# A hybrid decoder layer: PSUM tiles behind attention taken from the pool of the bank that the planner finds free, instead of from two pools in turn

## The chip, the cores and the metric

The kernel runs on one core of a Trainium2 chip. The engines named below are TensorE (PE, with PEld for its weight loads), VectorE (DVE), ScalarE (ACT), GpSimd (POOL) and SyncE (SP, which here only issues DMAs). TensorE writes its results to PSUM, which has eight banks; a tile of 128 x 512 float32 fills one bank. The metric is the time of one execution on the device in microseconds (us), the median of the runs.

## The reference

One layer of a hybrid decoder over 1024 positions of width 1024, in float32. Cut to what matters:

```python
h = rms_norm(x, norm_mix_pre)
q, k, v, cb, cc, cx, g_att, g_conv = split(h @ w_in)
o = stick_breaking_attention(heads(q), heads(k), heads(v))      # 8 heads of 64, causal
y_att = o @ w_att_branch
y_conv = (cb * causal_dwconv(cc * cx, conv_mix_w)) @ w_conv_branch
merged = sigmoid(g_att) * y_att + sigmoid(g_conv) * y_conv
x = x + rms_norm(merged @ w_out, norm_mix_post)
h = rms_norm(x, norm_ffn_pre)
a, g = split(causal_dwconv(h @ w_up, conv_ffn_w))                # 2 x 2816 columns
x = x + rms_norm((gelu(g) * a) @ w_down, norm_ffn_post)
```

## The kernel before

Every product is made of float16 halves: a float32 operand is split into a high and a low half, and three of the four products of halves are added up in PSUM, so that a product of 128 x 512 with an inner size of 512 is twelve matmuls (the three `PASSES` times four). The large products, up and down projection among them, go by a scheme of seven block products in place of eight, for which sums and differences of blocks of the activations and of the weights are made ahead.

The program has three parts, each put in order by a planner (`Plan`, at the end of the file). A part adds jobs (`pl.add`) with an engine, a cost, the tiles that they read and write and, for many, a due time; TensorE's large products keep the order in which they were added (`seq=True`), and the rest is fitted in. `Plan.order` walks a clock of its own, takes for each engine the job that can start first, and keeps for each pool of tiles a sorted list `free` of the times at which its buffers come free. The result is one fixed order for each engine. Which buffer a tile really gets is not part of the plan: when the program is written down, a job asks its pool for a tile (`Buf.t` calls `make`), the pool takes that one of its own buffers which comes free first in the library's own reckoning, and semaphore waits are added so that the new tile is not written before the last reader of the old one is through.

PSUM stands in two pools. While attention runs, `pm` (3 banks, L138) holds projections, and another pool holds attention's scores and outputs. Behind attention that other pool is closed, and `pz` (5 banks) takes its place; `pm` is kept as `self.pm3`. Both plans behind attention reckon with one pool `pm` of eight banks. The class `Ring` (L1815) joins the two for them: it has a list of eight entries, five times `pz` and three times `pm`, and each new tile is asked of the next entry, round and round, whatever that pool holds just then. `bank` (L739) is the one place where `rest` (the two parts behind attention) asks for a PSUM tile.

The stretch that matters below is the passage from the output projection to the up projection. The rows of the sequence stand in eight tiles of 128 positions, taken in the order 0, 4, 1, 5, 2, 3, 6, 7 (`TORDER`). For each tile, `out_proj` multiplies by `w_out` into two banks (`py`), adds the residual and makes the normed rows `hn`. Then the blocks of the activations that the up projection needs are made, in two ways:

- Tiles 3 and 7 are transposed on TensorE (L1317) into two banks, `pt`; for tile 7, ScalarE copies each into `hb` (L1357), and the differences `tb` are made from `hb`, split (L1350, L1351) and put into `hB` and `hT`.
- The others (`TURNED`) go through the DMA. For tiles 4, 5, 6 `heavy` (L1282) makes differences in two PSUM tiles `tp` on VectorE (L1289), ScalarE and VectorE split them into high and low halves in an SBUF tile `n` (L1270, L1271), and a transposing DMA from SyncE's queue puts each half into `hB` or `hT` (L1265). Two SBUF tiles `n` are used for a tile of positions; the first is written a second time after its first transposes were read.

The up projection takes its weights in 22 steps `u0` to `u21`. Each has raw weights (`ws_u`), a scale that goes through a one-column matmul `pr_u` (L813), four float16 weight tiles `wh_u` (L825 the high half on ScalarE, L827 the low half on VectorE), and three accumulators in PSUM: `pu0a`, `pu0b`, `pu0c` for step 0 (L1425). Products 1 and 2 of a step, into `b` and `a`, need only tiles 0 to 3; 5, 6, 7, 3 and 4 need blocks of tiles 4 to 7. For steps 0, 1 and 2 the products 1 and 2 are put ahead of the others (`PRE`), around the last transposes. TensorE's order there is: `pu1a`, transposes of tile 7 into `pt7_0` and `pt7_1`, `pu2b`, `pr_u` of step 3, `pu2a`, then `pu0c` (product 5) and twice `pu0b` (products 6 and 7).

Of the kernel before, what the change touches and what calls it, by code (L numbers as in the profile page):

```python
# [47 lines left out]
class Layer:  # L48
    def __init__(self, tc, a):
        self.tc, self.nc, self.a = tc, tc.nc, a  # L50
# [82 lines left out]
    def mixer(self, mid):  # L133
        tc, nc, a = self.tc, self.nc, self.a
        hT = self.hp.tile([P, 2, KD, T], F16, tag="hT", name="hT")
        with ExitStack() as ph1:
            pha = ph1.enter_context(ExitStack())
            pm = self.top.enter_context(tc.tile_pool(name="pm", bufs=3, space=bass.MemoryType.PSUM))  # L138
# [12 lines left out]
            if True:  # L151
# [34 lines left out]
                with tc.manual_schedule(engines={ET.PE, ET.DVE, ET.Activation, ET.SP, ET.Pool}):  # L186
# [3 lines left out]
                    vec, act, pe, pool = nc.vector, nc.scalar, nc.tensor, nc.gpsimd  # L190
                    NOTE = lambda: Buf(None, lambda: {})

                    def given(p, tile, avail=0.0):
                        b = Buf(p, None)
                        b.tile, b.avail = tile, avail
                        pl.caps[p] -= 1
                        return b
# [50 lines left out]
                    for c in range(2):  # L248
                        M(0.94, lambda c=c: pe.matmul(gpb.t.rearrange("p k t -> p (k t)")[:, ds(c * NH, NH)], on1[0:1, :],
                                                      gr[0:1, ds(c * NH, NH)], start=True, stop=True), [one_row, g_row], [(gpb, str(c))])  # L250
                    M(0.3, lambda: pe.matmul(ps2.t[:, 0:2], self.ones[0:1, :], g_c.t["g16"][0:1], start=True, stop=True),
                      [g_c], [ps2])
                    def norm(tt):
                        r, x = Buf("sm", lambda: self.small(f"r_pre{tt}")), xs[tt]
                        A(1.25, lambda: self.sumsq(xt[tt], r.t[:, 0:1], f"n_pre{tt}"), [x], [r])
                        V(0.15, lambda: vec.tensor_scalar(r.t[:, 1:2], r.t[:, 0:1], 1.0 / D, EPS, ALU.mult, ALU.add), [], [r])
                        pl.add("G", 0.6, lambda: pool.tensor_tensor(r.t[:, 2:3], r.t[:, 1:2], self.neghalf, ALU.pow), [], [r])
                        g = gpb if tt < 2 else gbb
                        V(1.28, lambda: vec.scalar_tensor_tensor(
                            xt[tt], xt[tt], r.t[:, 2:3], g.t.rearrange("p k t -> p (k t)") if tt < 2 else gb,  # L260
                            ALU.mult, ALU.mult), [r, g], [x])
# [412 lines left out]
                    for name in FILL:  # L674
                        which, j = name[:-1], int(name[-1])
# [5 lines left out]
                    k = 0  # L681
# [34 lines left out]
                    for b in [*(o16b[j] for j in range(4)), *(uf[j] for j in range(4)), *sig.values(), *(w for w, _ in wa), *yb.values(),  # L716
# [7 lines left out]

        self.xp = self.top.enter_context(tc.tile_pool(name="xp", bufs=4))
        self.h7p = self.top.enter_context(tc.tile_pool(name="h7p", bufs=1))
        self.pz = Ring((self.top.enter_context(tc.tile_pool(name="pz", bufs=5, space=bass.MemoryType.PSUM)), 5),
                       (self.pm3, 3))
        dram = self.dram = self.top.enter_context(tc.tile_pool(name="dram", bufs=1, space=bass.MemoryType.DRAM))
        self.x2 = [a["out"][ds(tt * P, P), :] for tt in range(self.DIRECT)] + \  # L730
            [dram.tile([P, D], F32, tag=f"x2_{tt}", name=f"x2d_{tt}") for tt in range(self.DIRECT, 8)]
# [3 lines left out]
    pz, DIRECT, dsums = None, 7, {}  # L735
# [1076 lines left out]
            pl.emit()  # L1812


class Ring:  # L1815


    def __init__(self, *pools):
        self.order, self.n = [p for p, k in pools for _ in range(k)], 0

    def tile(self, *a, **kw):
        p = self.order[self.n % len(self.order)]
        self.n += 1
        return p.tile(*a, **kw)


class Buf:
    def __init__(self, pool, make):
        self.pool, self.make, self.tile, self.log, self.left, self.avail = pool, make, None, [], 0, 0.0

    @property
    def t(self):
        if self.tile is None:
            self.tile = self.make()
        return self.tile

# [12 lines left out]
class Plan:  # L1849
# [29 lines left out]
    def order(self):  # L1879
        for j in reversed(self.jobs):  # L1880
            own = min([k.late for k in j.outs] + [j.due + j.lag + j.cost, self.now]) - j.lag - j.cost
            j.late = min(own, j.late) if j.seq else own
        free = {p: [0.0] * n for p, n in self.caps.items()}
        for j in self.jobs:
            j.n = len(j.deps)
            j.t0 = max([0.0] + [b.avail for b in j.bufs])
            for b in j.bufs:
                b.left += 1
                b.begun = b.tile is not None
        eng = {e: self.begin.get(e, 0.0) for e in self.LAG}  # L1890
        seq = [j for j in self.jobs if j.seq]
        pos = 0
        ready = {e: [j for j in self.jobs if j.eng == e and not j.n and not j.seq] for e in eng}
        dma, out, todo = self.loaded, [], len(self.jobs)
        while todo:
            best = None
            for e, now in eng.items():
                c = ready[e]
                if e == "PE" and pos < len(seq) and not seq[pos].n:
                    c = c + [seq[pos]]  # L1900
                pick = None
                for j in c:
                    t = max(now, j.t0 + j.rest, j.late - j.ahead)
                    for b in j.bufs:
                        if b.pool and not b.begun:
                            t = max(t, free[b.pool][0] + j.slack if free[b.pool] else 1e9)
                    key = (max(t, now + 0.05), j.late - (100 if e == "PE" and not j.seq else 0))
                    if t < 1e8:
                        if pick is None or key < pick[0]:
                            pick = key, t, j  # L1910
                if pick and (best is None or pick[1] < best[0]):
                    best = pick[1], e, pick[2]
            assert best, "no job can run"
            t, e, j = best
            todo -= 1
            if j.seq:
                pos += 1
            else:
                ready[e].remove(j)
            end = t + j.cost  # L1920
            eng[e] = end
            done = end + j.lag
            if hasattr(j, "load"):
                dma = max(dma, t + (1.9 if e == "SP" else 2.4)) + j.load
                done = dma + self.landed
            for b in j.bufs:
                if b.pool and not b.begun:
                    free[b.pool].pop(0)
                b.begun = True
                b.left -= 1  # L1930
                b.end = max(getattr(b, "end", 0.0), done)
                if b.pool and not b.left:
                    free[b.pool] = sorted(free[b.pool] + [b.end])
            for k in j.outs:
                k.n -= 1
                soon = self.own is not None and k.eng == e and not hasattr(j, "load")
                k.t0 = max(k.t0, end + self.own.get(e, 0.05) if soon else done if k.deps[j] else end)
                if not k.n and not k.seq:
                    ready[k.eng].append(k)
            out.append((t, len(out), j))  # L1940
        self.span, self.eng = max(eng.values()), eng
        return [j for _, _, j in sorted(out, key=lambda x: x[:2])]
# [46 lines left out]
```

## Time and profile before

| | |
|---|---|
| median of 3 runs | 1254.32 us (1254.06 to 1255.73) |
| profiled execution | 1258.49 us; its span, from first to last instruction, 1256.8 us |
| granted clock, mean over the span | 0.995 |
| ScalarE busy | 857.0 us, 68% |
| GpSimd busy | 86.1 us, 7% |
| HBM read and written | 92.88 MB and 37.75 MB |

The page's second part shows where in the span an engine is busy, in forty slices; a digit is the busy share in tenths. The twenty-first slice (about 628 to 660 us) holds the passage described above.

```profile
PE   9999999999999999999989999999999999999997
DVE  7988889857998675659869998699689869959866
PEclk9999999999999999999989999999999999999999
```

TensorE is busy almost throughout; the one digit below 9 ahead of the end is in that passage, and the granted clock dips in the same slice. Time that another engine stands idle costs nothing while TensorE is busy.

### The profile page before, as it was taken

To read this page: it belongs to the slowest core of one execution; us is meant where nothing else is said; L and a number is where in the kernel's file an instruction comes from. 1 tells how busy PE (TensorE), PEld (TensorE's weight loads), DVE (VectorE), ACT (ScalarE), POOL (GpSimd) and SP (SyncE) were. 2 spreads that over 40 slices of the span, in tenths; PEclk is the share of its full clock that TensorE was granted. 3 is DMA by queue.
4 is the path that set the end of the run, shared out by engine and by line. 5 is a ranking of instruction groups with operands and counts; after the bars stand their busy time and mean duration, and the time that the engine had idled before them with its cause. 6 is when DMAs were issued, how large, how long until landed. Compare 5 with 4: busy or idle time off the path is not lost.

```text
span 1256.8 us, 16464 instructions
## 1 busy us (share of the span) xinstructions
PE 1237.9 (98%) x6065; PEld 560.6 (45%) x6065; DVE 1014.5 (81%) x1599; ACT 857.0 (68%) x1250; POOL 86.1 (7%) x113
## 2 busy tenths in 40 slices
PE   9999999999999999999989999999999999999997
PEld 4444444444444444444434444444444444444443
DVE  7988889857998675659869998699689869959866
ACT  7766666736758465855647679678768967878424
POOL 1100000000000000002100001001200300111003
PEclk9999999999999999999989999999999999999999
DMA  8755677661223122657844105414930971594608
GB/s 277 158 135 104 143 134 177 150 135 35 67 84 118 34 73 70 227 168 167 220 116 137 61 14 212 190 34 82 251 103 6 200 197 34 94 257 140 180 1 134
DMA packets 148931, 160.80 MB, mean 128 GB/s; under 512 B 114425, under 2 KB 114553, under 8 KB 148850
## 3 DMA queue, kind: packets, MB, share of 16 engines
q1 hardware_dynamic: 138480, 123.05, 34.9%
q0 software_dynamic: 10368, 36.70, 14.1%
q8 instruction: 47, 0.77, 0.3%
q14 instruction: 34, 0.28, 0.1%
q10 hardware_dynamic: 2, 0.00, 0.0%
HBM read 92.88 MB, written 37.75 MB: 104 GB/s over the span
## 4 chain that ended last, share of the span: by engine, by line
PE 45%; DVE 2%; ACT 1%; issue 1%; DMA 1%; POOL 1%; POOLq 0%; DVEq 0%; ACTq 0%
PE pq L1584 12%; PE pd L1654 2%; PE pu2b L1425 1%; PE pu20b L1425 1%; PE pu19b L1425 1%; PE pu8b L1425 1%; PE pu6b L1425 1%; PE pu16b L1425 1%; PE pu12b L1425 1%; PE pu4b L1425 1%; PE pu3b L1425 1%; PE pu21b L1425 1%; PE pu13b L1425 1%; PE pu10b L1425 1%; PE pu18b L1425 1%
## 5 line engine op out<-in xcount | busy, mean ns | idle before, releaser
L1425 PEld LDWEIGHTS <-wh_u 128*128 128x128 f16 x1848 | 180.0, 98 | 222.6 <-issue 10.0
L825 ACT ACTIVATE wh_u<-ws_u,sc_u 128x1024 f16<-128x1024 f32 (+1 forms) x66 | 66.4, 1009 | 35.4 <-PE pr_dn L813 7.5
L994 PEld LDWEIGHTS <-wh_g 128*128 128x128 f16 x588 | 57.0, 98 | 68.9 <-issue 0.5
L1229 PE MATMUL py<-wo,m 128*128 128x512 f16 x384 | 83.3, 379 | 0.0
L1588 ACT ACTIVATE st<-pq,sd 128x512 f32<-128x512 f32 x112 | 74.8, 696 | 12.2 <-PE pq L1584 9.5
L827 DVE SCALAR_TENSOR_TENSOR wh_u<-ws_u,sc_u,wh_u 128x1024 f16<-128x1024 f32 (+1 forms) x66 | 72.5, 1104 | 10.2 <-ACT wh_u L825 9.7
L791 POOL DMA_DIRECT2D acc<-st x56 | 43.7, 781 | 435.8 <-ACT st L1588 435.8
L624 DVE TENSOR_TENSOR_SCAN e<-e,mask 128x512 f32<-128x512 f32 (+3 forms) x64 | 48.7, 808 | 13.3 <-ACT e L617 13.3
L1229 PEld LDWEIGHTS <-m 128*128 128x128 f16 x384 | 37.4, 98 | 44.9
L1457 DVE SCALAR_TENSOR_TENSOR ug<-cg,cw_g,ug 128x1023 f32<-128x1023 f32 (+1 forms) x44 | 56.3, 1279 | 1.3 <-ACT ug L1455 1.1
L1457 DVE SCALAR_TENSOR_TENSOR ua<-ca,cw_a,ua 128x1023 f32<-128x1023 f32 (+1 forms) x44 | 56.3, 1279 | 1.1 <-ACT ua L1455 1.1
L617 ACT ACTIVATE e<-z,cz 128x1024 f32<-128x1024 f32 (+3 forms) x48 | 42.2, 896 | 20.4 <-PE z L595 14.9
L66 ACT ACTIVATE jk_u<-ws_u 128x1024 bf16<-128x1024 f32 x44 | 46.5, 1056 | 11.8 <-DMA ws_u<-w_up_nt 11.7
L638 ACT ACTIVATE w<-e 128x1024 f16<-128x1024 f32 (+3 forms) x48 | 38.8, 837 | 12.6 <-DMA wt<-w 6.3
L459 PE MATMUL pcc<-hT,wh_cc 128*128 128x512 f16 x192 | 44.5, 380 | 0.8 <-ACT u L575 0.8
L459 PE MATMUL pk<-hT,wh_k 128*128 128x512 f16 x192 | 43.1, 379 | 0.0
L459 PE MATMUL pq<-hT,wh_q 128*128 128x512 f16 x192 | 43.0, 379 | 0.0
L1584 PE MATMUL pq<-wq,fx 128*128 128x512 f16 x192 | 42.8, 379 | 0.0
L1584 PE MATMUL pq<-wq,fy 128*128 128x512 f16 x192 | 42.7, 379 | 0.0
L924 PE MATMUL pywc<-p,wh_wc 128*128 128x512 f16 x192 | 42.6, 379 | 0.0
L1584 PE MATMUL pq<-wq,fs 128*128 128x512 f16 x192 | 42.2, 379 | 0.0
L624 DVE TENSOR_TENSOR_SCAN e<-e,cr,mask 128x512 f32<-128x512 f32 x32 | 39.8, 1273 | 1.0 <-ACT e L617 0.8
(795 smaller groups left out, 2734.0 us busy)
## 6 DMA issues: line engine op xcount, KB each, us to landing
acc<-st POOLq DMA_DIRECT2D x56, 512.0 KB, 6.1
ws_u<-w_up_nt SPq DMA_DIRECT2D x44, 512.0 KB, 3.6
ds<-w_down SPq DMA_DIRECT2D x18, 512.0 KB, 15.0
wt_g<-w_in_nt SPq DMA_DIRECT2D x14, 512.0 KB, 3.5
x<-x SPq DMA_DIRECT2D x8, 512.0 KB, 8.1
wr_wo<-w_out SPq DMA_DIRECT2D x8, 512.0 KB, 3.6
ws_wo<-w_out SPq DMA_DIRECT2D x8, 512.0 KB, 4.4
xr<-x SPq DMA_DIRECT2D x8, 512.0 KB, 4.5
```

Source lines behind the costliest of these rows:

```text
L66: self.nc.scalar.activation(self.junk(f"jk_{name}"), src, AF.Square, accum_out=acc)
L459: pe.matmul(ps.t, w.t[:, wi, ds(k * P, P)], hT[:, hi, k, ds(c * NH, NH)], start=k == 0 and p == 0, stop=k == KD - 1 and p == 2)
L624: vec.tensor_tensor_scan(x, x, m[:, ::-1], ONE if diag else cr.t[:, h:h + 1], ALU.mult, ALU.max)
L791: j = pl.add(eng, 0.45 if eng == "SP" else 1.14, lambda: e.dma_start(dst(), srcf(), **kw), r, [b] if w is None else w, ahead=AHEAD["load"] ...
L825: A(C["As" if big else "Ash"], lambda: act.activation(dst.t[:, 0, dsl], src.t[:, ssl], AF.Copy, scale=sb.t["s"]), [(src, sreg), sb], [(dst ...
L827: V(C["V" if big else "Vh"], lambda: vec.scalar_tensor_tensor(dst.t[:, 1, dsl], src.t[:, ssl], sb.t["s"], dst.t[:, 0, dsl], ALU.mult, ALU. ...
L994: pe.matmul(b.t, p.w[wt].t[:, wi, ds(wc * NH + k * P, P)], block(i, h, k), start=first and n == 0, stop=n == 3 * KH - 1, skip_group_check= ...
L1229: pe.matmul(b.t, m16[k].t[:, h_, ds(tt * P, P)], wo[k].t[:, w_, sl], start=k == 0 and p == 0, stop=k == 7 and p == 2)
L1425: pe.matmul(b.t, p.w[wt].t[:, wi, ds(wc * NH + k * P, P)], block(i, h, k), start=first and n == 0, stop=n == 3 * KH - 1, skip_group_check= ...
L1457: V(C["V"], lambda lag=lag: vec.scalar_tensor_tensor(u.t[:, lag:], c.t[:, :T - lag], sm.t[:, 2 - lag:3 - lag], u.t[:, lag:], ALU.mult, ALU ...
L1584: pe.matmul(b.t, fa[p].t[:, h, ds(fo * NH + tt * P, P)], wa[p].t[:, x, ds(wo * NH, NH)], start=first and n == 0, stop=n == 5, skip_group_c ...
L1588: A(C["Ah"], lambda tt=tt, b=b, st=st: act.activation(st.t[:, tt % 2, :], b.t, AF.Copy, scale=q.sd.t[:, 0:1]), [b, q.sd], [(st, str(tt % 2 ...
```

## The change

`Ring` goes. In its place, `Plan.order` keeps beside each free time of the pool `pm` which of the two PSUM pools the bank belongs to: five of the eight start as `pz` and three as `pm`. When a job takes a bank, the mark of the bank that came free first is stored in the tile's `Buf` (`which`), and when the tile is released the mark goes back into the list with the time. `Buf.t` sets `Banks.want` to that mark just before the tile is made, and `Banks.tile` asks that pool. Costs, due times and the free times are untouched.

```diff
-        self.pz = Ring((self.top.enter_context(tc.tile_pool(name="pz", bufs=5, space=bass.MemoryType.PSUM)), 5),
-                       (self.pm3, 3))
+        self.pz = Banks(self.top.enter_context(tc.tile_pool(name="pz", bufs=5, space=bass.MemoryType.PSUM)), self.pm3)
...
-class Ring:
+class Banks:
+    want = 0
     def __init__(self, *pools):
-        self.order, self.n = [p for p, k in pools for _ in range(k)], 0
+        self.pools = pools
     def tile(self, *a, **kw):
-        p = self.order[self.n % len(self.order)]
-        self.n += 1
-        return p.tile(*a, **kw)
+        return self.pools[Banks.want].tile(*a, **kw)
...
     def t(self):
         if self.tile is None:
+            Banks.want = self.which
             self.tile = self.make()
...
-        free = {p: [0.0] * n for p, n in self.caps.items()}
+        free = {p: [(0.0, p == "pm" and n == 8 and i > 4) for i in range(n)] for p, n in self.caps.items()}
...
-                            t = max(t, free[b.pool][0] + j.slack if free[b.pool] else 1e9)
+                            t = max(t, free[b.pool][0][0] + j.slack if free[b.pool] else 1e9)
...
-                    free[b.pool].pop(0)
+                    b.which = free[b.pool].pop(0)[1]
...
-                    free[b.pool] = sorted(free[b.pool] + [b.end])
+                    free[b.pool] = sorted(free[b.pool] + [(b.end, b.which)])
```

The order of instructions is the same on every engine, row by row. What differs in the built program is where 230 PSUM tiles lie, and with that the waits. (Line numbers behind the first edit are lower by one after the change.) In the passage described above the banks are these; a bank's former holder is the tile that must have been read before the new one is written:

| tile | bank, former holder, before | bank, former holder, after |
|---|---|---|
| `tp6_0` | 7 (`pz`), `py3_1` | 2 (`pm`), `tp5_0` |
| `tp6_1` | 5 (`pz`), `pr_u1` | 7 (`pz`), `pr_u1` |
| `pt7_0` | 3 (`pz`), `pr_u2` | 6 (`pz`), `pr_u2` |
| `pt7_1` | 3 (`pz`), `pt7_0` | 0 (`pm`), `pr_dn0` |
| `pu2b` | 3 (`pz`), `pt7_1` | 1 (`pm`), `pu0a` |
| `pr_u3` | 7 (`pz`), `tp6_0` | 6 (`pz`), `pt7_0` |
| `pu2a` | 1 (`pm`), `pr_dn0` | 0 (`pm`), `pt7_1` |
| `pu0c` | 2 (`pm`), `pu0a` | 2 (`pm`), `tp6_0` |

The first place is TensorE from the end of `pu1a` to the start of `pu2b`. A name in brackets is the semaphore that the row waits for: that of ScalarE (Activation), VectorE (DVE) or of a DMA queue. Before:

```order
L1425 MATMUL pu1a<-hT,wh_u_0_5767 128x512
L1317 MATMUL pt_0_5993<-ident,hn_5865 128x128 [waits DVE_49]
L1317 MATMUL pt_0_5993<-ident,hn_5865 128x128 x3
L1317 MATMUL pt_1_6001<-ident,hn_5865 128x128 [waits Activation_49]
L1317 MATMUL pt_1_6001<-ident,hn_5865 128x128 x3
L1425 LDWEIGHTS wh_u_0_5987
L1425 MATMUL pu2b<-hT,wh_u_0_5987 128x512 [waits Activation_49]
```

And after, where the wait of the second transposes is gone, the wait of `pu2b` is for VectorE (the reader of `pu0a`), and its weight's own wait, which the other had covered, stands by itself:

```order
L1424 MATMUL pu1a<-hT,wh_u_0_5767 128x512
L1316 MATMUL pt_0_5993<-ident,hn_5865 128x128 [waits DVE_49]
L1316 MATMUL pt_0_5993<-ident,hn_5865 128x128 x3
L1316 MATMUL pt_1_6001<-ident,hn_5865 128x128 x4
L1424 LDWEIGHTS wh_u_0_5987 [waits Activation_49]
L1424 MATMUL pu2b<-hT,wh_u_0_5987 128x512 [waits DVE_49]
```

In both, the third matmul of `pu2b` also waits for VectorE, for the low half of the weight. The second place is TensorE from the one-column product of step 3 (`pr_u`) to `pu0c`. Before:

```order
L813 LDWEIGHTS ones
L813 MATMUL pr_u_6032<-rb_u_5990,ones 128x1 [waits DVE_49]
L1425 LDWEIGHTS wh_u_0_5987
L1425 MATMUL pu2a<-hT,wh_u_0_5987 128x512
...
L1425 LDWEIGHTS wh_u_2_5268 [waits DMAHW5_49,DMAHW3_49]
L1425 MATMUL pu0c<-hB,wh_u_2_5268 128x512 [waits Activation_49]
L1425 LDWEIGHTS wh_u_2_5268 [waits DMAHW6_49]
L1425 MATMUL pu0c<-hB,wh_u_2_5268 128x512 [waits DMAHW4_49]
```

After:

```order
L812 LDWEIGHTS ones
L812 MATMUL pr_u_6032<-rb_u_5990,ones 128x1 [waits Activation_49]
L1424 LDWEIGHTS wh_u_0_5987
L1424 MATMUL pu2a<-hT,wh_u_0_5987 128x512 [waits Activation_49]
...
L1424 LDWEIGHTS wh_u_2_5268 [waits DMAHW5_49,DMAHW3_49]
L1424 MATMUL pu0c<-hB,wh_u_2_5268 128x512 [waits DVE_49]
L1424 LDWEIGHTS wh_u_2_5268 [waits DMAHW6_49]
L1424 MATMUL pu0c<-hB,wh_u_2_5268 128x512 [waits DMAHW4_49]
```

`pr_u` waits for ScalarE's copy of `pt7_0` in place of VectorE's last reading of `tp6_0`; that reading is now what the first matmul of `pu0c` waits for. The DMA waits, for the transposes of tile 6, are the same.

The library also gives some SBUF tiles of the pool of weights another buffer, since its reckoning of free times has changed. The third place is ScalarE where it fills the second SBUF tile `n` of tile 6 (`n_6_6057`; `n_6_5999` is the first). Before, it lay in the buffer of the first and waited for the DMAs that read that:

```order
L1350 ACTIVATE hB<-tb_0_6026 128x4x128 [waits DVE_49]
L1270 ACTIVATE n_6_5999<-tp_0_5886 128x512 [waits DMAHW3_49]
L1270 ACTIVATE n_6_6057<-tp_1_5888 128x512 [waits DMAHW5_49,DMAHW6_49,DMAHW4_49,DVE_49]
L1270 ACTIVATE n_6_6057<-hn_5755 128x512
L1350 ACTIVATE hB<-tb_1_6059 128x4x128 [waits DVE_49]
L1434 ACTIVATE cg_5930<-pu0c 128x512 [waits PE_49]
L825 ACTIVATE wh_u_2_6097<-s_u_5911,sc_u_5881 128x1024
```

After, it lies where the first weight tile of step 2 was and waits for TensorE's last use of that, the end of `pu2a`; the wait for the DMAs has gone to a weight tile of step 2 (`wh_u_2_6097`), four rows further on:

```order
L1349 ACTIVATE hB<-tb_0_6026 128x4x128 [waits DVE_49]
L1269 ACTIVATE n_6_5999<-tp_0_5886 128x512 [waits DMAHW3_49]
L1269 ACTIVATE n_6_6057<-tp_1_5888 128x512 [waits DVE_49,PE_49]
L1269 ACTIVATE n_6_6057<-hn_5755 128x512
L1349 ACTIVATE hB<-tb_1_6059 128x4x128 [waits DVE_49]
L1433 ACTIVATE cg_5930<-pu0c 128x512 [waits PE_49]
L824 ACTIVATE wh_u_2_6097<-s_u_5911,sc_u_5881 128x1024 [waits DMAHW5_49,DMAHW6_49,DMAHW4_49,Activation_49]
```

In both, VectorE's third filling of `n_6_5999` (L1271, the last reader of `tp6_0`) waits for the DMA that transposes what it overwrites.

More of the change, by code (lines that the diff above doesn't have):

```diff
@@ L1812, in rest @@
             pl.emit()
-class Ring:
+class Banks:
+    want = 0
     def __init__(self, *pools):
-        self.order, self.n = [p for p, k in pools for _ in range(k)], 0
+        self.pools = pools
     def tile(self, *a, **kw):
-        p = self.order[self.n % len(self.order)]
-        self.n += 1
-        return p.tile(*a, **kw)
+        return self.pools[Banks.want].tile(*a, **kw)
 class Buf:
     def __init__(self, pool, make):
-        self.pool, self.make, self.tile, self.log, self.left, self.avail = pool, make, None, [], 0, 0.0
+        self.pool, self.make, self.tile, self.log, self.left, self.avail, self.which = pool, make, None, [], 0, 0.0, 0
     @property
```

## The prediction

> **What bounds the kernel now.** I read the page's first part, then TensorE's waits, then the stretch in which they lie.
>
> ```profile
> span 1256.8 us, 16464 instructions
> ...
> PE 1237.9 (98%) x6065; PEld 560.6 (45%) x6065; DVE 1014.5 (81%) x1599; ACT 857.0 (68%) x1250; POOL 86.1 (7%) x113
> ```
>
> TensorE sets the time: the span holds 1256.8 − 1237.9 = 18.9 us in which it is not busy. The list of TensorE's waits (total, times, longest) has these entries behind attention that concern banks:
>
> ```profile
> PE pt L1317 <- ACT hb L1357: 2.6, 1, 2.6
> PE pr_u L813 <- DVE n L1271: 2.5, 1, 2.5
> ...
> PE pu0b L1425 <- ACT ca L1434: 0.7, 1, 0.7
> PE pu2b L1425 <- ACT hb L1357: 0.7, 1, 0.7
> ...
> PE pg6c L994 <- ACT cgg L1006: 0.2, 1, 0.2
> ```
>
> `hb` and `n` are no inputs of what waits for them: they read the tile that held the bank before (the table of banks above). `pu0b` and `pg6c` wait for copies of their own accumulator; those waits stay. The timeline of TensorE (start, duration; in brackets the idle time before it) shows where they stand:
>
> ```profile
> 638.02 2.75 PE L1425 MATMUL pu1a<-hT,wh_u 128*128 128x512 f16 x12
> 640.61 0.60 PE L1317 MATMUL pt<-ident,hn 128*128 128x128 f32 x4
> 643.85 1.11 PE L1317 MATMUL pt<-ident,hn 128*128 128x128 f32 x4 [2.64 <-ACT hb L1357]
> 645.65 5.13 PE L1425 MATMUL pu2b<-hT,wh_u 128*128 128x512 f16 x12 [0.68 <-ACT hb L1357]
> 653.30 0.16 PE L813 MATMUL pr_u<-rb_u,ones 128*128 128x1 bf16 x1 [2.53 <-DVE n L1271]
> 653.33 4.44 PE L1425 MATMUL pu2a<-hT,wh_u 128*128 128x512 f16 x12
> 657.60 2.75 PE L1425 MATMUL pu0c<-hB,wh_u 128*128 128x512 f16 x12
> 660.19 2.75 PE L1425 MATMUL pu0b<-hB,wh_u 128*128 128x512 f16 x12
> 663.63 2.75 PE L1425 MATMUL pu0b<-hB,wh_u 128*128 128x512 f16 x12 [0.68 <-ACT ca L1434]
> ```
>
> From the first transposes to `pu0c` pass 657.60 − 640.61 = 17.0 us. Twelve matmuls take 640.61 − 638.02 = 2.59 us at full clock, 0.216 us each; `pu2b` took 5.13. The windows (length, PE, PEld, DVE and ACT busy, PEclk near the end) say why:
>
> ```profile
> 111.18:114.59 3.41, 2.29 (x13) 0.70 (x11) 3.41 (x6) 3.41 (x6) 0.00 (x0) 1.00 1.02 194
> ...
> 640.25:643.66 3.41, 0.96 (x7) 0.53 (x5) 1.59 (x4) 3.41 (x6) 0.00 (x0) 1.00 0.14 58
> 643.66:650.49 6.83, 5.96 (x16) 2.57 (x17) 4.30 (x8) 1.89 (x4) 0.00 (x0) 0.50 0.42 80
> 650.49:653.90 3.41, 0.88 (x6) 0.31 (x4) 1.89 (x3) 1.60 (x3) 0.00 (x0) 1.00 0.07 15
> 653.90:657.32 3.42, 3.42 (x10) 1.22 (x8) 0.43 (x1) 1.06 (x3) 0.00 (x0) 0.50 0.31 62
> 657.32:700.00 42.68, 42.00 (x197) 19.01 (x196) 40.21 (x58) 31.28 (x43) 0.00 (x0) 1.00 0.35 114
> 700.00:1200.00 500.00, 500.00 (x2342) 226.86 (x2341) 423.96 (x621) 380.03 (x528) 49.61 (x63) 1.00 0.49 129
> ```
>
> Each hole is followed by a half clock, for 6.83 and 3.42 us: a stretch of 3.41 us with TensorE busy for 0.96 or 0.88 lowered it, one with 2.29 did not. From 700 to 1200 TensorE is busy without a break, so what is won before 657 stays won unless another engine cannot follow.
>
> **What the change does to this stretch.** By the rows of the instruction order above nothing moves on any engine, DMA queues of SyncE and GpSimd included; about fifty waits differ. Elsewhere the tiles change places among banks that are free anyway, and I cost that at nothing: the 0.2 us of `pg6c` is all that TensorE waits there, so there is nothing to gain, and the new neighbours were read 3 us or more before, so nothing to lose. So I follow the stretch with the waits of the new rows, and need ScalarE, VectorE and the DMA transposes of tile 6:
>
> ```profile
> 641.21 1.13 ACT L825 ACTIVATE wh_u<-ws_u,sc_u 128x1024 f16<-128x1024 f32 x1
> 642.25 1.06 ACT L1270 ACTIVATE n<-tp 128x512 f16<-128x512 f32 x2
> 643.20 0.59 ACT L1357 ACTIVATE hb<-pt 128x512 f32<-128x512 f32 x1
> ...
> 650.81 0.60 ACT L1434 ACTIVATE cg<-pu2b 128x512 f32<-128x512 f32 x1 [4.03 <-PE pu2b L1425]
> 651.30 0.62 ACT L1350 ACTIVATE hB<-tb 128x512 f16<-128x512 f32 x1
> 651.82 0.59 ACT L1270 ACTIVATE n<-tp 128x512 f16<-128x512 f32 x1
> 656.26 0.60 ACT L1270 ACTIVATE n<-tp 128x512 f16<-128x512 f32 x1 [3.85 <-DMA hB<-n]
> ```
>
> ```profile
> 642.38 1.28 DVE L827 SCALAR_TENSOR_TENSOR wh_u<-ws_u,sc_u,wh_u 128x1024 f16<-128x1024 f32 x1 [0.69 <-ACT wh_u L825]
> ...
> 651.96 0.69 DVE L1351 TENSOR_TENSOR hB<-tb,hB 128x512 f16<-128x512 f32 x1 [3.85 <-ACT hB L1350]
> 652.57 0.68 DVE L1271 TENSOR_TENSOR n<-tp,n 128x512 f16<-128x512 f32 x1
> ...
> 656.89 0.69 DVE L1271 TENSOR_TENSOR n<-tp,n 128x512 f16<-128x512 f32 x1 [3.04 <-ACT n L1270]
> ```
>
> ```profile
> 644.89 1.23 SPq L1265 DMA_TRANSPOSE hB<-n  x1
> ```
>
> ```profile
> DMA to landing us min/median/max: 5.1/5.1/5.1
> ```
>
> (the last line is for that one transpose.)
>
> 1. The second four transposes lose their wait: they follow at 641.2 and end by 641.8 (0.60 a group).
> 2. `pu2b` loses the bank's wait, and what is late next is its weight: ScalarE's half is there at 642.34, VectorE's at 642.38 + 1.28 = 643.66, which the third matmul needs. Two matmuls run at 642.4, ten from 643.7: 10 × 0.216 = 2.16, end 645.9.
> 3. `pr_u` now waits for the copy that ends at 643.79, which is past. `pu2a` waits for the second copy, on ScalarE right behind the first (644.4), past too: 2.59, end 648.5.
> 4. `pu0c` gets a wait that it did not have, for VectorE's third `n` (L1271), since it now fills the bank of `tp6_0`. That instruction overwrites what the transpose issued at 644.89 reads, so it starts at 644.89 + 5.1 = 649.99 at the earliest and ends at 650.7. The queue ahead of it does not hold it longer: with `pu2b` done at 645.9, ScalarE's `cg`, `hB` and `n` (0.5 to 0.6 each) end by about 647.7. `pu0c` itself needs the data of that same transpose, so without the new wait it would start at 650.0; the wait's price is 0.7 us. Behind it in TensorE's queue stands everything else; VectorE and ScalarE meanwhile work ahead.
> 5. `pu0c` so starts at 650.7 instead of 657.60: **6.9 us** earlier.
>
> Can the rest follow? VectorE is busy for 40.21 of the 42.68 us behind 657.32 and could be the next bound; but its idle 3.85 and 3.04 us above, 6.9 together, belong to this knot and go with it: the first hangs on ScalarE's `cg` behind `pu2b`, the second on ScalarE's `n`, which waited for DMA since its SBUF buffer was that of the transposes' source. In the new rows this `n` has the buffer of `pu2`'s first weight and waits for `pu2a` (648.5) instead. Queued behind it on ScalarE are `n`, `hB` and the copy of `pu0c`, wanted by the second `pu0b` at about 656.5; VectorE's third `n`, at 650.7, and some four instructions of 0.7 us lead there by about 653.5, so 3 us of cover are left. The weight that now waits for those DMAs instead is used by products that run from 684 on.
>
> **The sum.** Against the profiled execution's own time: 1258.49 − 6.9 = 1251.6 us, if its clock steps are typical. The runs' median, 1254.32, lies 4.2 us below that execution, and the clock of those runs is not recorded. So I take the 6.9 apart. Without any half clock before, the second transposes would take 0.60, `pu2b` end at 647.7, `n` on VectorE still end at 650.7, and `pu0c` start at 650.7 + 2.6 = 653.3: then 2.6 us are won. With the first half clock alone `pu0c` starts at 653.30 + 2.6 = 655.9: 5.2 us. With both: 6.9. New holes of 0.6, 0.9 and 2.2 us (648.5 to 650.7) remain, and a half clock behind the last would cost half of 3.41, 1.7 us. The edges of the clock's stretches fall elsewhere in each execution: between the first transposes and `pu2b` lie 5.0 us with 1.7 of transposes, more than one stretch, so the first drop comes nearly always but may hit less of `pu2b`; I take the middle of 2.6 and 5.2, 3.9. The second hole is shorter than a stretch: half of 1.7, 0.85. The new one is shorter still: a quarter of 1.7, 0.4. 3.9 + 0.85 − 0.4 = 4.3 us, **1250.0 us** against the median; own range 1247.4 (6.9) to 1251.7 (2.6).
>
> **Rivals.** First, a small gain. If the timed runs of before had no half clock, or the hole of 2.2 us now brings one, 2.6 to 0.9 us are left, 1251.7 to 1253.4. For it speaks that the median lies so far under the profiled time; against it, that both holes lowered the clock here. [...] Chance 0.17.
>
> Second, slower: the new wait of `pu0c`. It decides as soon as VectorE's `n` ends behind 657.6, and from there each us costs one. It would take a transpose that lands 12 us after its issue instead of 5.1, because it now runs beside transposes issued earlier than before; then 2.5 us more make 1257. No row comes near that. Chance 0.05.
>
> Third, the waits go but do not matter, or a bank picked by the plan's clock is not the one free on the chip, and the holes stay: 1254.3. The new rows show the waits gone. Chance 0.03.
>
> **How the numbers follow.** The forecast has 0.75. Within 0.2% (2.5 us, about what a measurement of this kernel can tell from no change) lie the first and third rival, 0.20; slower 0.05. The range runs from 1247.2 to 1252.8, into the first rival's times.
>
> **What would show it.** The list of TensorE's waits has no `pt` and no `pr_u` entry of 2.5 us; `pu2b` waits under 1 us twice, for `wh_u`; `pu0c` waits about 2 us for VectorE's `n` or the transpose; from first transposes to `pu0c` pass some 10 us instead of 17.0; ScalarE's idle 4.03 and 3.85 us shrink. It is wrong if `pu0c` waits longer than 3 us, if a half clock lies on it, or if TensorE waits for a weight behind 660.

## The result, and the profile after

| | before | after |
|---|---|---|
| median | 1255.73 us (1254.06 to 1258.61, 7 runs) | 1250.72 us (1249.10 to 1251.73, 7 runs) |
| after / before | | 0.9958 (95% interval 0.9945 to 0.9970) |
| profiled execution | 1258.49 us | 1251.30 us |
| granted clock, mean | 0.995 | 0.998 |

The change makes the kernel faster by 0.42%, 5.0 us; the forecast was 1250.0. The first part of the page of after:

```profile
span 1249.6 us, 16464 instructions
...
PE 1233.4 (99%) x6065; PEld 559.1 (45%) x6065; DVE 1014.4 (81%) x1599; ACT 857.7 (69%) x1250; POOL 86.0 (7%) x113
```

The span is 7.2 us shorter; TensorE's busy time is 4.5 us less, though it does the same matmuls, and its idle time 2.7 less (18.9 before, 1249.6 − 1233.4 = 16.2 now). The same work took less busy time because the clock was higher: its mean rose from 0.995 to 0.998. The list of TensorE's waits after (total, times, longest):

```profile
PE pu0c L1424 <- DVE n L1270: 1.6, 1, 1.6
PE pu2b L1424 <- ACT wh_u L824: 1.0, 1, 1.0
...
PE pu2b L1424 <- DVE wh_u L826: 0.7, 1, 0.7
PE pu0b L1424 <- ACT ca L1433: 0.7, 1, 0.7
```

The two waits of 2.6 and 2.5 us, for the readers of a bank's former holder, are gone. `pu2b` now waits for what it reads, its weight `wh_u`; the one wait for the reader of a bank's former holder that is left in the passage is the new one of `pu0c`. The timeline of TensorE in the passage (start, duration, in brackets the idle time before):

```profile
640.52 1.04 PE L1316 MATMUL pt<-ident,hn 128*128 128x128 f32 x8
642.53 0.61 PE L1424 MATMUL pu2b<-hT,wh_u 128*128 128x512 f16 x2 [0.98 <-ACT wh_u L824]
643.85 2.33 PE L1424 MATMUL pu2b<-hT,wh_u 128*128 128x512 f16 x10 [0.71 <-DVE wh_u L826]
646.02 0.17 PE L812 MATMUL pr_u<-rb_u,ones 128*128 128x1 bf16 x1
646.05 2.75 PE L1424 MATMUL pu2a<-hT,wh_u 128*128 128x512 f16 x12
650.41 2.75 PE L1424 MATMUL pu0c<-hB,wh_u 128*128 128x512 f16 x12 [1.61 <-DVE n L1270]
```

From the first transposes to `pu0c` pass 650.41 − 640.52 = 9.9 us; they were 17.0. The start of `pu0c` comes 657.60 − 650.41 = 7.2 us earlier, and that is all of the difference of the spans. From `pu0c` to the last group of the down projection pass 588.2 us in both profiles (657.60 to 1245.81, and 650.41 to 1238.62), so nothing is won or given back behind the passage. The windows over the two holes that are left (length, then busy times of PE, PEld, DVE and ACT, the granted clock third from the end):

```profile
641.35:644.76 3.41, 1.72 (x9) 0.55 (x8) 2.56 (x5) 3.38 (x7) 0.00 (x0) 1.00 0.02 4
...
648.18:651.59 3.41, 1.80 (x9) 0.78 (x8) 2.34 (x5) 2.13 (x4) 0.00 (x0) 1.00 0.19 39
```

Both stretches keep the full clock, and so do those behind them (1.00 from 651.59 to 655.00, and over all of 655 to 1240). Last, ScalarE and then VectorE ahead of `pu0c`:

```profile
648.00 0.60 ACT L1269 ACTIVATE n<-tp 128x512 f16<-128x512 f32 x1 [0.54 <-DMA hB<-n]
648.84 0.60 ACT L1269 ACTIVATE n<-tp 128x512 f16<-128x512 f32 x1 [0.24 <-PE pu2a L1424]
```

```profile
649.67 0.69 DVE L1270 TENSOR_TENSOR n<-tp,n 128x512 f16<-128x512 f32 x1 [1.07 <-DMA hB<-n]
```

ScalarE's idle stretch of 4.03 us ahead of `cg` is gone, with 0.54 us left two rows later, ahead of the first of these `n`; the 3.85 us ahead of the second are down to 0.24. VectorE's third `n`, which `pu0c` waits for, starts when the transpose has landed (in brackets 1.07 us for the DMA).

### The profile page after: what moved, and what is told of

Same layout as the page of the kernel before. It is cut to its first block, busy times and chain, and to the rows that moved or that the text cites. A ratio compares the mean times of both kernels' runs of the same rounds, so it can differ in the third digit from the quotient of the medians.

```text
span 1249.6 us, 16464 instructions
## 1 busy us (share of the span) xinstructions
PE 1233.4 (99%) x6065; PEld 559.1 (45%) x6065; DVE 1014.4 (81%) x1599; ACT 857.7 (69%) x1250; POOL 86.0 (7%) x113
## 4 chain that ended last, share of the span: by engine, by line
PE 45%; DVE 3%; issue 1%; ACT 1%; POOL 1%; DMA 1%; POOLq 0%; DVEq 0%; ACTq 0%
PE pq L1583 12%; PE pd L1653 2%; PE pu6b L1424 1%; PE pu4b L1424 1%; PE pu20b L1424 1%; PE pu19b L1424 1%; PE pu16b L1424 1%; PE pu12b L1424 1%; PE pu8b L1424 1%; PE pu21b L1424 1%; PE pu18b L1424 1%; PE pu17b L1424 1%; PE pu15b L1424 1%; PE pu14b L1424 1%; PE pu13b L1424 1%
## 5 line engine op out<-in xcount | busy, mean ns | idle before, releaser
L826 DVE SCALAR_TENSOR_TENSOR wh_u<-ws_u,sc_u,wh_u 128x1024 f16<-128x1024 f32 (+1 forms) x66 | 72.5, 1104 | 10.3 <-ACT wh_u L824 9.8
```

Source lines behind the costliest of these rows:

```text
L826: V(C["V" if big else "Vh"], lambda: vec.scalar_tensor_tensor(dst.t[:, 1, dsl], src.t[:, ssl], sb.t["s"], dst.t[:, 0, dsl], ALU.mult, ALU. ...
```

## The experiments

The theory under test: TensorE was held by two waits, each for the reader of a bank's former holder; each hole (a stretch in which TensorE stands idle) also halved TensorE's clock behind it in some executions; and with both gone, the transposes of tile 6 and the third `n` behind them are what is late next. The rivals: one of the two holes makes the whole gain (A); it comes from other tiles' banks or from the SBUF buffers (B); the half clock is not brought by the holes (C); only the number of waits counts (D); VectorE sets the time behind 657 (E). The runs were made in three jobs, each with runs of before beside it: 28, 17 and 11. Ratios are against these, since the medians of before (1257.10, 1257.97 and 1256.62) differ by job. A ratio's interval is the 95% one.

### One hole at a time, and both

In these kernels `bank` gives the tiles named a bank from the pool named, and leaves all else to the ring as before. Entry 7 of `pz.order` is `pm`, entry 0 is `pz`.

```diff
+    MOVED = {'pt7_1': 7}
     def bank(self, name):
+        if name in self.MOVED:
+            self.pz.n += 1
+            return self.pz.order[self.MOVED[name]].tile([P, NH], F32, tag="pm", name=name)
         return self.pz.tile([P, NH], F32, tag="pm", name=name)
```

The second kernel has `{'pr_u3': 7, 'pu0c': 0}`, the third all three entries.

> The kernel before with one tile moved: the second half of tile 7's transposes, pt7_1, gets a free bank instead of the bank of pt7_0. My theory (each bank wait holds TensorE by itself, and the next late thing takes its place): the hole of 2.6 us ahead of the second transposes goes, pu2b runs from 642.4 to 645.9, but pr_u3 still fills the bank of tp6_0 and now waits for VectorE's third n until about 650.7, a hole of 4.8 us; pu2a then ends at 653.3 and pu0c starts at 653.4 with a full clock, at up to 655.9 with a half clock behind the hole: 1.7 to 4.2 us less than before, two thirds of the change's gain at most. Rival A (the first hole makes the whole gain): pu0c at about 650.5, 5 us less by the median. Rival B (the gain comes from other tiles' banks or the SBUF buffers): no difference.

> The kernel before with two tiles moved: pr_u3 gets a free bank, and pu0c takes the bank behind tp6_0 that pr_u3 had. My theory: the hole of 2.6 us at the second transposes and the half clock on pu2b stay, pu2b ends at about 650.8; pr_u3 follows without its 2.5 us, pu2a runs at full clock to 653.4, and pu0c starts at about 653.4 instead of 657.6: 4.2 us less in the profile, some 3.4 to 4.2 by the median. Rival A (the first hole makes the whole gain): under 1 us. Rival B (other tiles' banks or the SBUF buffers): no difference.

> The kernel before with the three tiles of the two runs above moved together, and all other banks and the SBUF buffers as before. My theory: the whole gain of the change, pu0c at about 650.5, some 7 us less in the profile and 5 us less by the median; but ScalarE's n still has the SBUF buffer of the transposes' source, so 0.5 us of it may be missing. Rival B (other tiles' banks or the SBUF buffers): less than 1 us of the 5.

| moved | median | ratio to before (95%) | `pu0c` starts at (profile) |
|---|---|---|---|
| `pt7_1` | 1256.55 us (11 runs) | 0.9991 (0.9982 to 1.0000) | 655.26 |
| `pr_u3`, `pu0c` | 1253.92 us (11 runs) | 0.9979 (0.9968 to 0.9990) | 653.62 |
| all three | 1251.42 us (5 runs) | 0.9952 (0.9938 to 0.9966) | 650.61 |

The first, in TensorE's timeline:

```profile
640.44 1.04 PE L1322 MATMUL pt<-ident,hn 128*128 128x128 f32 x8
643.99 4.44 PE L1430 MATMUL pu2b<-hT,wh_u 128*128 128x512 f16 x12 [2.52 <-ACT hb L1362]
650.96 0.16 PE L818 MATMUL pr_u<-rb_u,ones 128*128 128x1 bf16 x1 [2.53 <-DVE n L1276]
650.99 4.44 PE L1430 MATMUL pu2a<-hT,wh_u 128*128 128x512 f16 x12
655.26 2.75 PE L1430 MATMUL pu0c<-hB,wh_u 128*128 128x512 f16 x12
```

My expectation of `pu2b` at 642.4 missed. With `pt7_1` out of bank 3, it is `pu2b` that follows `pt7_0` there, so the same copy, `hb`, is waited for, one step later: 2.52 us in place of 2.64. Saved in the profile is mainly what stood between the two in before, the second transposes and the wait of 0.68 us for their copy (`pu2b` starts 3.55 us behind the first transposes and not 5.04); another 0.7 us comes from a `pu2b` that ran less of its time at half clock, 4.44 us in place of 5.13. `pr_u` waits for VectorE's `n` as before, and both halves of the passage lie behind a drop of the clock, as its windows show:

```profile
641.17:644.58 3.41, 0.89 (x6) 0.45 (x5) 2.37 (x5) 3.38 (x8) 0.00 (x0) 1.00 0.00 0
644.58:648.00 3.42, 3.42 (x10) 1.22 (x8) 3.42 (x6) 1.14 (x2) 0.00 (x0) 0.50 1.21 143
648.00:651.41 3.41, 0.88 (x5) 0.31 (x4) 1.81 (x4) 1.60 (x3) 0.00 (x0) 1.00 0.10 23
```

So moving the first tile alone moves the wait instead of taking it away. In the profile `pu0c` starts 2.3 us earlier than in before, but by the ratio only 0.09% is won, 1.1 us, with an interval that reaches 1, where I expected 1.7 to 4.2 us: all its eleven runs have a mean clock of 0.996 or 0.997, while some of before's have more (below). The second kernel came out nearly as the theory has it: the first hole (3.35 us in this profile) and the half clock on `pu2b` stay, the hole of 2.5 us and the second half clock go. Its median lies 3.2 us under that of before, by the ratio 2.6 us, a little less than the 3.4 to 4.2 expected:

```profile
644.12 1.11 PE L1322 MATMUL pt<-ident,hn 128*128 128x128 f32 x4 [3.35 <-ACT hb L1362]
645.91 5.18 PE L1430 MATMUL pu2b<-hT,wh_u 128*128 128x512 f16 x12 [0.69 <-ACT hb L1362]
650.92 0.17 PE L818 MATMUL pr_u<-rb_u,ones 128*128 128x1 bf16 x1
650.95 2.75 PE L1430 MATMUL pu2a<-hT,wh_u 128*128 128x512 f16 x12
653.62 2.75 PE L1430 MATMUL pu0c<-hB,wh_u 128*128 128x512 f16 x12
```

Rival A falls: by the ratios the two alone have 0.09% and 0.21% of the 0.48% that all three have, and neither interval reaches that of all three. The second has more of the gain than the first (by the medians 3.2 of 5.7 us). With all three tiles moved the ratio is that of the change, so B falls for the other tiles' banks, as far as these intervals reach. (The library shifted 46 later tiles, too, so that 49 of 421 PSUM tiles differ from before and not 230. The SBUF buffer of `n` moved along in this run and in the one before it, which I had not expected, so on the SBUF half of B they do not speak.) The timeline of the third kernel holds a surprise:

```profile
643.66 4.42 PE L1430 MATMUL pu2b<-hT,wh_u 128*128 128x512 f16 x12 [2.32 <-ACT hb L1362]
647.87 0.21 PE L818 MATMUL pr_u<-rb_u,ones 128*128 128x1 bf16 x1
647.95 2.76 PE L1430 MATMUL pu2a<-hT,wh_u 128*128 128x512 f16 x12
650.61 2.75 PE L1430 MATMUL pu0c<-hB,wh_u 128*128 128x512 f16 x12
```

Here `pu2b` still waits 2.32 us for `hb` and still meets a half clock, 4.42 in place of 2.75. It costs next to nothing: `pu0c` starts at 650.61, behind `pu2a` without a wait, against 650.41 after a wait of 1.61 in the change; from the first transposes that is 10.3 against 9.9 us. The stretch that dropped the clock there:

```profile
641.17:644.59 3.42, 1.10 (x7) 0.54 (x6) 2.69 (x6) 3.39 (x6) 0.00 (x0) 1.00 0.06 13
```

Once `pr_u` is free, the first hole and its half clock fit into the time for which `pu0c` must wait anyway.

### The holes filled

All banks as before; the products added are never read.

```diff
+    def fill(self, n):
+        b = self.pm3.tile([P, NH], F32, tag="pm", name="fill", bufs=3)
+        for _ in range(n):
+            self.nc.tensor.matmul(b, self.hT[:, 0, 0, :P], self.hT[:, 0, 0, :NH], start=True, stop=True)
...
+                    if tt == 7 and e == 0:
+                        self.fill(10)
...
+                if (f, i) == (2, 1):
+                    self.fill(12)
```

> The kernel before, all banks as before, with products that nothing reads in the two holes, into a bank that is free: ten matmuls of 128x512 (2.2 us) behind pt7_0's transposes and twelve (2.6 us) behind pu2b. TensorE so waits as long for the banks but is busy meanwhile. My theory of the clock's share (the holes lower the clock behind them): no half clock; the second transposes still at 643.9, pu2b ends at 648.3, pr_u3 waits for VectorE's n until about 651, pu0c starts at about 653.6: 4 us less in the profile and up to 4 us by the median, in spite of 4.8 us of added products. Rival C (the half clock stretches come by themselves, whatever TensorE does): the half clock stays and the time is that of before or up to 1 us more.

Measured: 1253.63 us (1253.30 to 1255.63, 11 runs), ratio 0.9976 (0.9966 to 0.9985). In its timeline every product runs at the full clock:

```profile
640.38 0.60 PE L1322 MATMUL pt<-ident,hn 128*128 128x128 f32 x4
640.82 2.32 PE L745 MATMUL fill<-hT 128*128 128x512 f16 x10
643.50 0.66 PE L1322 MATMUL pt<-ident,hn 128*128 128x128 f32 x4 [0.36 <-ACT hb L1364]
644.84 2.75 PE L1432 MATMUL pu2b<-hT,wh_u 128*128 128x512 f16 x12 [0.69 <-ACT hb L1364]
647.43 2.75 PE L745 MATMUL fill<-hT 128*128 128x512 f16 x12
650.15 2.75 PE L1432 MATMUL pu2a<-hT,wh_u 128*128 128x512 f16 x12
652.74 2.75 PE L1432 MATMUL pu0c<-hB,wh_u 128*128 128x512 f16 x12
```

22 products more, and 0.24% faster: rival C falls. This kernel waits for the banks as before did and has the clock of after, so it parts the gain. What is left to the waits alone is the way from it to the change: the passage, from the first transposes to `pu0c`, has 652.74 − 640.38 = 12.4 against 9.9 us, 2.5 more. The medians give 1253.63 − 1250.72 = 2.9 us, but from two jobs; within one job, against the kernel with three tiles moved, they give 1253.63 − 1251.42 = 2.2. The rest of the gain is the clock's.

### The bank behind tp6_0 one product earlier

`MOVED = {'pt7_1': 7, 'pu2b': 7, 'pu2a': 0}`: `pt7_1`, `pu2b` and `pr_u3` wait for no late reader, as in the change, but `pu2a` gets the bank behind `tp6_0`, which `pu0c` has there.

> The kernel before with three tiles moved so that the first hole goes as in the change (pt7_1 and pu2b in free banks, pr_u3 behind pt7_0), but the bank behind tp6_0 is filled by pu2a, one product earlier than in the change, where pu0c fills it. The number of waits is that of the change. My theory (the bank wait at pu0c is cheap only because pu0c needs the transposes' data at about the same time, and whoever waits for VectorE's third n stops until about 650.4): pu2b ends at about 646, pu2a starts at about 650.4 and pu0c at 653.0, or up to 654.7 with a half clock behind the hole of 4.4 us: 2.4 to 4.3 us more than the change, 1253.1 to 1255. Rival D (what counts is that the first hole is gone and the waits are few): the time of the change, 1250.7 to 1251.4.

Measured: 1255.75 us (1253.51 to 1258.05, 12 runs), ratio 0.9981 (0.9970 to 0.9991). The timeline:

```profile
649.75 4.25 PE L1430 MATMUL pu2a<-hT,wh_u 128*128 128x512 f16 x12 [4.34 <-DVE n L1276]
653.84 2.75 PE L1430 MATMUL pu0c<-hB,wh_u 128*128 128x512 f16 x12
```

Rival D falls. The same wait, one product earlier in the queue, stops TensorE for 4.34 us and brings back a half clock (4.25 us for `pu2a` in place of 2.75); 0.19% is won in place of 0.42%. The median lies above the 1253.1 to 1255 that I expected. In the change it stands at the product that could not have started much earlier, since its data come by the same transposes. (`pu0c` starts 3.4 us later than in the change and the profiled execution, 1254.74 us, is 3.4 us longer than that of after. Why the slowest of the twelve took 1258.05 us stays open.)

### Bringing forward what is late next

In after, TensorE's waits hang on ScalarE, which stands idle for the DMA of step 3's raw weights before it sums their squares (`jk_u`), with `wh_u` and `n` queued behind:

```profile
640.29 1.06 ACT L66 ACTIVATE jk_u<-ws_u 128x1024 bf16<-128x1024 f32 x1 [2.53 <-DMA ws_u<-w_up_nt]
```

One line of the planner's input puts these sums later:

```diff
-                    A(C["Aq"], lambda e=e, b=b: self.sumsq(b.t, sq.t[:, e:e + 1], f"{n}_{e}"), [b], [sq], ahead=aq)
+                    A(C["Aq"], lambda e=e, b=b: self.sumsq(b.t, sq.t[:, e:e + 1], f"{n}_{e}"), [b], [sq], ahead=aq).rest = 2.0 * (f == 3)
```

> The change, and the sums of squares of the up projection's fourth weight group are planned 2 us later, so that ScalarE scales the third group's first weight and makes tile 6's n before the sum that waits 2.5 us for its DMA, and pu0c fills the bank of pt7_1 instead of that of tp6_0; some of ScalarE's and VectorE's order changes to the end of the span. My theory: pu2b starts behind the transposes at about 641.5 without a wait, n is made from 641.4, its transposes land 1 us earlier, and pu0c, without a bank wait, starts at 648 to 649.3: 1 to 2.4 us less than the change, 1248.3 to 1249.7. Rival E (from 657 on VectorE sets the time, which is busy for over nine tenths there): no gain over the change, 1250.7 or more.

> As the kernel above with 4 us: the sum of squares goes behind n and the copies of tile 7's transposes, pr_u3 behind pu0c and two further products, and pu0c fills the bank of pt7_0. My theory: n is made from 640.5 on, its transposes land at about 648, pu0c starts at about 648: 2 to 2.4 us less than the change, 1248.3 to 1248.7, unless the fourth group's scale, which comes later, makes its first product wait. Rival E: no gain over the change.

> The later sums of squares of 2 us alone, with the banks given out as before the change. If the order alone heals the holes, the time is that of the same order with the changed banks, about 1249; my theory is that pu2b still waits for the copy of pt7_0 and pt7_1 now for the reader of pu1a, so that a bank wait of 1 to 3 us and a half clock remain: 1251 to 1256.

| kernel | median (6 runs each) | ratio to before (95%) |
|---|---|---|
| change, 2 us later | 1247.99 us | 0.9923 (0.9910 to 0.9936) |
| change, 4 us later | 1248.04 us | 0.9922 (0.9908 to 0.9935) |
| before, 2 us later | 1249.00 us | 0.9933 (0.9918 to 0.9947) |

TensorE in the first of them (ScalarE starts the weight `wh_u` at 637.85 there and at 641.35 in after):

```profile
640.24 1.04 PE L1316 MATMUL pt<-ident,hn 128*128 128x128 f32 x8
641.11 2.75 PE L1424 MATMUL pu2b<-hT,wh_u 128*128 128x512 f16 x12
643.70 2.75 PE L1424 MATMUL pu2a<-hT,wh_u 128*128 128x512 f16 x12
...
646.32 0.38 PE L1424 MATMUL pu0c<-hB,wh_u 128*128 128x512 f16 x1
646.98 2.55 PE L1424 MATMUL pu0c<-hB,wh_u 128*128 128x512 f16 x11 [0.28 <-DMA hB<-n]
```

The passage is closed: `pu0c` starts 6.1 us behind the first transposes, and what it waits for is its data, 0.28 us. That is earlier than the 648 to 649.3 that I expected, and the time is a little under the 1248.3 to 1249.7. With 4 us, the first matmul of `pu0c` starts at 646.92, the others wait 1.36 us for their data, and the time is the same. Rival E falls in the first profile: behind 657 VectorE follows. Beside the change itself, on one chip, the first of the three was run again:

> The change once more, beside the next kernel on the same chip. Expected 1250 to 1252; if its clock is granted as in the first seven runs (0.998 or 0.999), no half clock falls on the passage behind attention.

> The change with the later sums of squares of 2 us once more, beside the change itself: if the 3 us between the two in separate jobs are the kernels' own, 1247.5 to 1248.5, 2.5 to 3.5 us less than the change; if they came from the chip, no difference.

The change: 1250.54 us (1249.25 to 1251.60, 6 runs), ratio 0.9956 (0.9942 to 0.9970). With 2 us: 1249.34 us (1247.38 to 1250.31, 6 runs), ratio 0.9943 (0.9926 to 0.9960). So the advantage over the change was 1.2 us here and not 3, and these two intervals overlap: it beats before in both jobs, but by how much it beats the change, and so whether E is wholly wrong, is not settled. The passage is shorter in both of its profiles, but in the second not all of it is kept: `pu0c` ends 2.7 us earlier than in the change beside it, and the span is only 0.6 us shorter. The line also reorders ScalarE and VectorE to the end of the span, and a later wait of TensorE, 0.3 us in its first profile, took this in the second:

```profile
PE pu14b L1424 <- ACT ca L1433: 1.3, 1, 1.3
```

The third of the table was a miss: with the banks of before the later sums alone give 1249.0, where I expected 1251 to 1256. In that order tile 7's second transposes wait for another reader, for less long, and up to `pu0c` nothing waits behind them; no clock drops (`pu2b`, `pu2a` and `pu0c` take 2.75 us each). (`pt7_1` lies behind `pu1a` here, whose reader `ca` ends on VectorE at 642.28; the `sc_u` that the profile names reads no bank and ends just behind it.)

```profile
642.34 0.66 PE L1317 MATMUL pt<-ident,hn 128*128 128x128 f32 x4 [1.66 <-DVE sc_u L803]
...
648.04 2.75 PE L1425 MATMUL pu0c<-hB,wh_u 128*128 128x512 f16 x12
```

With this order the change of banks is worth about 1 us, the third row of the table against the first, with intervals that overlap, so it can't be told from nothing: the ring's harm depended on which jobs happened to stand around the last transposes.

## Why the prediction came true, and where it was off

**Steps 1 to 3** hold to 0.3 us. The transposes end at 640.52 + 1.04 = 641.56 (forecast 641.8); `pu2b`'s two parts start at 642.53 and 643.85 (642.4, 643.7); `pr_u` follows at 646.02 (645.9); `pu2a` ends at 650.41 − 1.61 = 648.80 (648.5).

**Step 4**, the new wait of `pu0c`: forecast from 648.5 to 650.7, measured from 648.80 to 650.41. Its price, 0.7 us, is supported but not shown apart: `n` starts at 649.67 as the transpose lands (forecast 649.99), which `pu0c` needs too, and `pu0c` starts 0.74 later. That the place of the wait decides is shown by the run with `pu2a` there.

**Step 5**: 6.9 forecast, 7.2 measured in the profiles. That the banks of the other tiles cost and win nothing is what the run with three tiles moved shows, within its interval.

**The cover** of ScalarE's `n`, which now waits for `pu2a`: it starts at 648.84, 0.24 late, and TensorE has no wait behind it but the old one of `pu0b`, 0.7. In the kernels above in which that `n` still waited for the DMA (the first tile alone, the holes filled, `pu2a` behind `tp6_0`) the passage brought TensorE no further wait either. But there `n` started between 1.6 us ahead of `pu0c` and 0.4 us behind it. In the change the old buffer would put it 2.5 to 3 us behind: in these kernels it follows the end of VectorE's third `n`, 650.36 in after, by 2.5 to 3.0 us. By ScalarE's rows that would make the second `pu0b` about 1 us later, an estimate. No run has the change's banks with the old buffer, so whether the buffer is part of the gain is not shown.

**The term that was mis-sized is the clock's.** The prediction took the 4.2 us between the profiled execution and the median of three for a clock that hits `pu2b` more or less, and blended: 3.9 + 0.85 − 0.4 = 4.3. It held that the first drop "comes nearly always". The 56 runs of before beside the experiments fall into two groups instead:

| granted clock, mean of the span | runs | median | range |
|---|---|---|---|
| 0.995 to 0.997 | 40 | 1257.92 us | 1256.02 to 1259.97 |
| 0.998 or 0.999 | 16 | 1254.22 us | 1253.74 to 1256.19 |

The profiled execution, 1258.49 at 0.995, is of the upper group, and the first three runs (1254.06 to 1255.73) lie in the lower one by their times. So against the upper group the change wins 1257.92 − 1250.72 = 7.2 us, the 6.9 of step 5; against the lower 3.5, for which I had 2.6 (3.5 also within the third job, 1254.03 − 1250.54); between the groups lie 3.7. So, by the clock, the drop was missing in 16 of 56 runs, and, by their times, in all three that the forecast started from: its 1.3 and 0.85 us for the clock had nothing to act on there. The 2.6 for the waits alone agrees with the filled kernel (2.2 to 2.9), but is 0.9 less than the way from the lower group; why that group is 0.6 us slower than the filled kernel stays open. The deduction of 0.4 for a new half clock was for nothing, since the stretches with the new holes keep their clock. These errors mostly cancelled: 4.3 was taken off 1254.32, of which 3.6 came true. The mechanism was right; that the forecast time came within 0.7 us is in part luck. Which of its executions meet the half clock, only profiles show; none of the lower group was taken, so that its passage has no half clock is inferred from the mean clock and the filled kernel. The edges of the clock's stretches did fall elsewhere in each profile that has this drop: the first half clock begins 3.05 us behind the start of the first transposes in before (640.61 to 643.66), and 4.14, 3.86 and 4.28 us behind it with the first tile (640.44 to 644.58), the other two (640.17 to 644.03) and all three moved (640.31 to 644.59). That this is what parts the runs of before into two groups is a guess; no run shows it.

**The rivals.** The first, a small gain because the timed runs of before had no half clock, had its premise right for the three runs that were shown, and not for most: in 40 of 56 the clock was lower. Its time, 1251.7 to 1253.4, was too high by 1.0 at its lower end, since against such runs the change won 3.5 and not 2.6, and no new drop came; the forecast was nearer by only 0.3 us. What it set against itself, that the holes of before lowered the clock, was seen again in the experiments: the clock fell behind holes of 2.32 us (all three moved) and 2.52 us (the first alone), as behind the 2.64 us of before, in stretches with 1.10, 0.89 and 0.96 us of work. The second, `pu0c`'s wait, was 1.61 us and far from its point of 657.6. The third did not happen.

## What to carry to other kernels

When a wait names an engine whose result the waiting instruction does not read, look up which tile held its buffer before: the cure is another buffer, at no cost in instructions. But place the late reader's buffer under the product that must wait for late data anyway: the same wait stopped TensorE for 4.3 us one product earlier, and its own price at the right one is an estimated 0.7, and moving one tile by itself only passed the wait on. Where times of one program form two groups, compare the granted clock of the runs before working from a median of three.

## What the runs showed of the hardware

In these profiles the clock changes in steps of 3.41 us: in before it falls at 643.66, returns at 650.49, falls at 653.90 and returns at 657.32, which are 6.83, 3.41 and 3.42 us apart; with `pt7_1` moved it changes at 644.58, 648.00, 651.41 and 654.82. Stretches with TensorE busy for 0.88 and 0.96 us (before), 0.88 and 0.89 (`pt7_1` moved) and 1.10 (all three moved) were followed by a half clock; those with 2.29 (before, 111.18 to 114.59) and with 1.72 and 1.80 (after) were not. (The stretches of after are counted back in the same steps from its drop at 1245.5, and that of before back from its own at 643.66.) The windows of the kernel with `pr_u3` and `pu0c` moved show what I had not expected of the way back:

```profile
640.62:644.03 3.41, 0.15 (x2) 0.00 (x0) 1.70 (x4) 3.41 (x6) 0.00 (x0) 1.00 0.07 29
644.03:647.45 3.42, 2.65 (x8) 1.41 (x9) 3.27 (x6) 1.78 (x4) 0.00 (x0) 0.50 0.73 140
647.45:650.86 3.41, 3.41 (x9) 1.22 (x8) 0.92 (x2) 0.00 (x0) 0.00 (x0) 0.50 0.09 21
```

At half clock a stretch with 2.65 us busy was followed by another at half clock; behind one with 3.41 the clock returned. In the run with `pu2a` behind `tp6_0` it was whole again behind this one, with 3.06 us busy (`pu0c`, from 653.84, takes 2.75 us):

```profile
649.41:652.82 3.41, 3.06 (x8) 1.11 (x8) 0.89 (x2) 0.57 (x2) 0.00 (x0) 0.50 0.32 64
```

At full clock a stretch with 1.72 us, in after, had been followed by another at full clock. In before, too, the first half clock lasted for two stretches, 6.83 us, where a second wait of 0.68 us lay in the first of them, with 2.54 us busy.
